# Batch normalisation of 32 x 256 x 128 x 128: two neighbouring channels per partition, 64 KB rows and a three-slot buffer

## Chip, cores, metric

One core of one Trainium2 chip. The metric is the device time of one execution in microseconds. This program runs on one core.

## The reference

```python
x: (32, 256, 128, 128) float32;  gamma, beta, running_mean, running_var: (256,)
out = gamma * (x - mean) / np.sqrt(var + 1e-5) + beta     # per channel
```

Mean and variance are inputs, so for each channel this is one multiplication and one addition. 537 MB are read and 537 MB are written.

## The kernel before

Scale and bias are worked out once per channel tile of 128 channels. The main loop then moves tiles of 128 partitions x 8192 elements (32 KB a partition, 4 MB in all) through three buffers. ScalarE does the multiplication and addition in place. SyncE issues all transfers: an issue takes it 0.34 to 0.45 us in the main loop, and the transfer is carried out later by 16 DMA engines (a load lands 22.5 us after its issue on median). The code below is cut (`...`) and its calls are drawn together on one line.

```python
x_v = x.rearrange("n (ct p) h w -> n ct p (h w)", p=P)     # channel = ct * 128 + p
...
for ct in range(c_tiles):                    # 2: eight parameter loads of 128 x 1
    nc.sync.dma_start(out=g_sb, in_=g_v[ct].unsqueeze(1))
    ...                                      # beta, mean, variance; then scale and bias
CHUNK = 8192                                 # 32 KB a partition (worked out in the kernel)
pool = ctx.enter_context(tc.tile_pool(name="sbuf", bufs=3))
for ni in range(n):
    for ct in range(c_tiles):
        for ck in range(num_chunks):         # 2
            t = pool.tile([P, CHUNK], f32, tag="t")
            nc.sync.dma_start(out=t, in_=x_v[ni, ct, :, lo:hi])                 # L88
            nc.scalar.activation(out=t, in_=t, func=Ident, bias=bias_sb, scale=scale_sb)   # L89
            nc.sync.dma_start(out=out_v[ni, ct, :, lo:hi], in_=t)               # L96
```

The scheduler of the language chooses the order in which SyncE issues these transfers. It is not the order of the loop, as the timeline below shows.

## Time and profile before

| | |
|---|---|
| time, median of 5 | 2520.67 us (2517.77 to 2531.01) |
| span of the profiled run | 2516.0 us |
| DMA queue | 99.9% of 16 engines' span, 427 GB/s |
| ScalarE | 37% busy |
| VectorE | 0% busy |

These lines are from the page of the kernel before: busy time by engine, GB/s in 40 slices of the span, the DMA queue's share, the costliest group of instructions, and the DMA issues with their size and the median time from issue to landing.

```profile
span 2516.0 us, 713 instructions
DVE 1.5 (0%) x10; ACT 924.8 (37%) x131; POOL 0.2 (0%) x4
...
GB/s 392 432 427 431 421 431 428 431 433 427 431 425 426 426 432 429 429 426 425 433 426 425 431 428 425 425 425 426 425 433 425 426 433 425 426 433 427 432 429 413
...
q1 hardware_dynamic: 38016, 1073.76, 99.9%
...
L89 ACT ACTIVATE t<-t,bias_sb,scale_sb 128x8192 f32<-128x8192 f32 x128 | 923.2, 7212 | 1573.5 <-DMA t<-in_x_dram 1573.5
...
t<-in_x_dram SPq DMA_DIRECT2D x128, 4096.0 KB, 22.5
out_dram<-t SPq DMA_DIRECT2D x128, 4096.0 KB, 12.2
```

From the first packet of x, 5.5 us into the span, the DMA engines are recorded busy practically all the time (99.9%). In the main loop ScalarE waits for loads and for nothing else (1573.5 us in 128 waits). And a store lands 12.2 us after its issue, although its own bytes take 9.7 us (8 packets of 1213 ns on each engine).

SyncE's timeline of the kernel before (start, duration, engine, line, operation, tile; SPq is SyncE; a merged line spans first to last):

```profile
3.52 0.43 SPq L53 DMA_DIRECT2D m_sb<-in_running_mean_dram  x1
4.00 0.43 SPq L54 DMA_DIRECT2D v_sb<-in_running_var_dram  x1
4.47 0.91 SPq L88 DMA_DIRECT2D t<-in_x_dram  x2
24.09 9.96 SPq L96 DMA_DIRECT2D out_dram<-t  x2
34.10 2.40 SPq L88 DMA_DIRECT2D t<-in_x_dram  x2
```

The order is two loads, two stores, two loads. The parameter loads take SyncE until 4.47 us.

Below the views lie the packet records: a packet is here one record of the DMA trace, a piece of a transfer on one engine. 94% of the 32 KB packets took 1213 ns, within 5 ns. What packets took above that is called **excess** below: summed and divided by 16 engines. In this profile it was 26.5 us.

### The profile page before, as it was taken

The page shows a single profiled execution, that of the slowest core. Times are in us where ns is not written, and L with a number is a line of the kernel's source. Part 1 is how long each engine was busy: PE and PEld are TensorE (multiplying, and loading weights), DVE is VectorE, ACT ScalarE, POOL GpSimd, SP SyncE. Part 2 cuts the span into 40 slices and gives each one's busy share as a digit, 9 for nine tenths or more (in the row PEclk, how much of TensorE's full clock was granted, in tenths as well). Part 3 has the DMA queues.
Part 4 walks back from the last instruction along what each step waited for, and adds up shares of the span by engine and source line. Part 5 has one row for each costly group of instructions (what it writes and reads, how often), then busy time and mean ns, then how long its engine had stood idle before and what let it go on. Part 6 is the DMA issues. An engine that isn't in the chain of part 4 may idle for free.

```text
span 2516.0 us, 713 instructions
## 1 busy us (share of the span) xinstructions
DVE 1.5 (0%) x10; ACT 924.8 (37%) x131; POOL 0.2 (0%) x4
## 2 busy tenths in 40 slices
DVE  0000000000000000000000000000000000000000
ACT  3342433424334243342433433334243342332433
POOL 0000000000000000000000000000000000000000
DMA  9999999999999999999999999999999999999999
GB/s 392 432 427 431 421 431 428 431 433 427 431 425 426 426 432 429 429 426 425 433 426 425 431 428 425 425 425 426 425 433 425 426 433 425 426 433 427 432 429 413
DMA packets 38021, 1073.80 MB, mean 427 GB/s; under 512 B 5248, under 2 KB 5248, under 8 KB 5248
## 3 DMA queue, kind: packets, MB, share of 16 engines
q1 hardware_dynamic: 38016, 1073.76, 99.9%
q14 instruction: 5, 0.04, 0.0%
HBM read 536.88 MB, written 536.87 MB: 427 GB/s over the span
## 4 chain that ended last, share of the span: by engine, by line
DMA 80%; ACT 18%; SPq 1%; issue 0%; ACTq 0%
DMA t<-in_x_dram 65%; ACT t L89 18%; DMA out_dram<-t 15%; SPq L96 0%; ACTq L89 0%; SPq L54 0%; SPq L53 0%; SPq L52 0%; SPq L51 0%; SPq L88 0%
## 5 line engine op out<-in xcount | busy, mean ns | idle before, releaser
L89 ACT ACTIVATE t<-t,bias_sb,scale_sb 128x8192 f32<-128x8192 f32 x128 | 923.2, 7212 | 1573.5 <-DMA t<-in_x_dram 1573.5
L60 ACT ACTIVATE v_sb<-v_sb 128x1 f32<-128x1 f32 x2 | 0.4, 202 | 4.0 <-DVE v_sb L59 4.0
L60 ACT ACT_TABLE_LOAD x1 | 1.3, 1283 | 0.7 <-PEq L111 0.7
L61 DVE RECIPROCAL v_sb<-v_sb 128x1 f32<-128x1 f32 x2 | 0.3, 164 | 0.3 <-ACT v_sb L60 0.3
L64 DVE TENSOR_TENSOR bias_sb<-b_sb,m_sb 128x1 f32<-128x1 f32 x2 | 0.3, 159 | 0.1
L63 DVE TENSOR_TENSOR m_sb<-m_sb,scale_sb 128x1 f32<-128x1 f32 x2 | 0.3, 159 | 0.0
L62 DVE TENSOR_TENSOR scale_sb<-g_sb,v_sb 128x1 f32<-128x1 f32 x2 | 0.3, 158 | 0.1
L59 DVE TENSOR_SCALAR v_sb<-v_sb 128x1 f32<-128x1 f32 x2 | 0.3, 154 | 5.3 <-DMA v_sb<-in_running_var_dram 5.3
L111 POOL MEMSET const-bfloat16-1.0<- 128x1 bf16 x1 | 0.1, 101 | 0.0
L111 POOL MEMSET const-uint8-127<- 128x1 uint8 x1 | 0.1, 101 | 0.0
L111 POOL MEMSET const-float32-0.0<- 128x1 f32 x1 | 0.1, 98 | 0.2 <-issue 0.2
L111 POOL MEMSET const-float32-1.0<- 128x1 f32 x1 | 0.1, 98 | 0.0
## 6 DMA issues: line engine op xcount, KB each, us to landing
t<-in_x_dram SPq DMA_DIRECT2D x128, 4096.0 KB, 22.5
out_dram<-t SPq DMA_DIRECT2D x128, 4096.0 KB, 12.2
g_sb<-in_gamma_dram SPq DMA_DIRECT2D x2, 0.5 KB, 2.0
b_sb<-in_beta_dram SPq DMA_DIRECT2D x2, 0.5 KB, 2.1
m_sb<-in_running_mean_dram SPq DMA_DIRECT2D x2, 0.5 KB, 2.0
v_sb<-in_running_var_dram SPq DMA_DIRECT2D x2, 0.5 KB, 2.0
```

What stands on the lines that cost most here:

```text
L59: nc.vector.tensor_scalar_add(out=v_sb, in0=v_sb, scalar1=float(eps))
L60: nc.scalar.sqrt(out=v_sb, in_=v_sb)
L61: nc.vector.reciprocal(out=v_sb, in_=v_sb)
L62: nc.vector.tensor_mul(out=scale_sb, in0=g_sb, in1=v_sb)
L63: nc.vector.tensor_mul(out=m_sb, in0=m_sb, in1=scale_sb)
L64: nc.vector.tensor_sub(out=bias_sb, in0=b_sb, in1=m_sb)
L89: nc.scalar.activation(out=t, in_=t, func=Ident, bias=bias_sb, scale=scale_sb,)
L111: nc = _bacc.Bacc("TRN2", target_bir_lowering=False, num_devices=1)
```

## The change

The intent is longer contiguous rows, fewer and larger transfers, and fewer parameter loads. Channels 2p and 2p+1 go to partition p, so one partition's two channels are 128 KB in a row in memory. Three slots of 64 KB a partition replace three buffers of 32 KB. Where two adjacent slots are next, a whole image (16 MB) loads in one transfer. Otherwise its two channel tiles load one by one.

```diff
-    g_v = gamma.rearrange("(ct p) -> ct p", p=P)
+    g_v = gamma.rearrange("(p ct) -> p ct", p=P)
     ... (beta, mean, variance likewise)
+    x_v = x.rearrange("n (p ct) h w -> n ct p (h w)", p=P)
+    out_v = out.rearrange("n (p ct) h w -> n ct p (h w)", p=P)
-    for ct in range(c_tiles):
-        g_sb = scratch.tile([P, 1], f32, tag=f"g{ct}")
-        nc.sync.dma_start(out=g_sb, in_=g_v[ct].unsqueeze(1))
+    g_sb = scratch.tile([P, c_tiles], f32, tag="g")
+    nc.sync.dma_start(out=g_sb, in_=g_v)
     ... (four parameter loads in place of eight; same arithmetic on 128 x 2)
-    pool = ctx.enter_context(tc.tile_pool(name="sbuf", bufs=3))
+    NSLOTS = 3
+    pool = ctx.enter_context(tc.tile_pool(name="sbuf", bufs=1))
+    big = pool.tile([P, NSLOTS, hw], f32)
+    x_p = x.rearrange("n (p two) h w -> n p (two h w)", two=2)
+    slot = 0
     for ni in range(n):
+        if slot + 2 <= NSLOTS:
+            t = big[:, slot:slot + 2, :]
+            nc.sync.dma_start(out=t, in_=x_p[ni].rearrange("p (two m) -> p two m", two=2))
+            for ct in range(2):
+                nc.scalar.activation(out=big[:, slot + ct, :], ...)      # 128 x 16384
+                nc.sync.dma_start(out=out_v[ni, ct], in_=big[:, slot + ct, :])
+            slot = (slot + 2) % NSLOTS
+        else:
+            for ct in range(2):
+                ...    # load, activation, store of one slot (the very last one in two halves)
+                slot = (slot + 1) % NSLOTS
```

More of the change, by code (lines that the diff above doesn't have):

```diff
@@ L31 @@
     out_v = out.rearrange("n (ct p) h w -> n ct p (h w)", p=P)
-    g_v = gamma.rearrange("(ct p) -> ct p", p=P)
-    b_v = beta.rearrange("(ct p) -> ct p", p=P)
-    rm_v = running_mean.rearrange("(ct p) -> ct p", p=P)
-    rv_v = running_var.rearrange("(ct p) -> ct p", p=P)
+    g_v = gamma.rearrange("(p ct) -> p ct", p=P)
+    b_v = beta.rearrange("(p ct) -> p ct", p=P)
+    rm_v = running_mean.rearrange("(p ct) -> p ct", p=P)
+    rv_v = running_var.rearrange("(p ct) -> p ct", p=P)
+    x_v = x.rearrange("n (p ct) h w -> n ct p (h w)", p=P)
+    out_v = out.rearrange("n (p ct) h w -> n ct p (h w)", p=P)
     f32 = mybir.dt.float32
@@ L41 @@
     scratch = ctx.enter_context(tc.tile_pool(name="scratch", bufs=1))
-    scale_aps = []
-    bias_aps = []
-    for ct in range(c_tiles):
-        g_sb = scratch.tile([P, 1], f32, tag=f"g{ct}")
-        b_sb = scratch.tile([P, 1], f32, tag=f"b{ct}")
-        m_sb = scratch.tile([P, 1], f32, tag=f"m{ct}")
-        v_sb = scratch.tile([P, 1], f32, tag=f"v{ct}")
-        nc.sync.dma_start(out=g_sb, in_=g_v[ct].unsqueeze(1))
-        nc.sync.dma_start(out=b_sb, in_=b_v[ct].unsqueeze(1))
-        nc.sync.dma_start(out=m_sb, in_=rm_v[ct].unsqueeze(1))
-        nc.sync.dma_start(out=v_sb, in_=rv_v[ct].unsqueeze(1))
-        scale_sb = params.tile([P, 1], f32, tag=f"scale{ct}")
-        bias_sb = params.tile([P, 1], f32, tag=f"bias{ct}")
-        nc.vector.tensor_scalar_add(out=v_sb, in0=v_sb, scalar1=float(eps))
-        nc.scalar.sqrt(out=v_sb, in_=v_sb)
-        nc.vector.reciprocal(out=v_sb, in_=v_sb)
-        nc.vector.tensor_mul(out=scale_sb, in0=g_sb, in1=v_sb)
-        nc.vector.tensor_mul(out=m_sb, in0=m_sb, in1=scale_sb)
-        nc.vector.tensor_sub(out=bias_sb, in0=b_sb, in1=m_sb)
-        scale_aps.append(scale_sb)
-        bias_aps.append(bias_sb)
@@ L69 @@
-    CHUNK = hw
-    MAX_BYTES_PER_PART = 32 * 1024
-    while CHUNK * 4 > MAX_BYTES_PER_PART:
-        CHUNK //= 2
-    assert hw % CHUNK == 0
-    num_chunks = hw // CHUNK
-    pool = ctx.enter_context(tc.tile_pool(name="sbuf", bufs=3))
+    g_sb = scratch.tile([P, c_tiles], f32, tag="g")
+    b_sb = scratch.tile([P, c_tiles], f32, tag="b")
+    m_sb = scratch.tile([P, c_tiles], f32, tag="m")
+    v_sb = scratch.tile([P, c_tiles], f32, tag="v")
+    nc.sync.dma_start(out=g_sb, in_=g_v)
+    nc.sync.dma_start(out=b_sb, in_=b_v)
@@ new lines @@
+    nc.sync.dma_start(out=m_sb, in_=rm_v)
+    nc.sync.dma_start(out=v_sb, in_=rv_v)
+    scale_full = params.tile([P, c_tiles], f32, tag="scale")
+    bias_full = params.tile([P, c_tiles], f32, tag="bias")
+    nc.vector.tensor_scalar_add(out=v_sb, in0=v_sb, scalar1=float(eps))
+    nc.scalar.sqrt(out=v_sb, in_=v_sb)
+    nc.vector.reciprocal(out=v_sb, in_=v_sb)
+    nc.vector.tensor_mul(out=scale_full, in0=g_sb, in1=v_sb)
+    nc.vector.tensor_mul(out=m_sb, in0=m_sb, in1=scale_full)
+    nc.vector.tensor_sub(out=bias_full, in0=b_sb, in1=m_sb)
@@ L78 @@
+    scale_aps = [scale_full[:, ct:ct + 1] for ct in range(c_tiles)]
+    bias_aps = [bias_full[:, ct:ct + 1] for ct in range(c_tiles)]
+    assert c_tiles == 2, "optimized for 256 channels"
+    NSLOTS = 3
+    pool = ctx.enter_context(tc.tile_pool(name="sbuf", bufs=1))
+    big = pool.tile([P, NSLOTS, hw], f32)
     Ident = mybir.ActivationFunctionType.Identity
+    x_p = x.rearrange("n (p two) h w -> n p (two h w)", two=2)
+    out_p = out.rearrange("n (p two) h w -> n p (two h w)", two=2)
+    slot = 0
@@ L80 @@
     for ni in range(n):
-        for ct in range(c_tiles):
-            scale_sb = scale_aps[ct]
-            bias_sb = bias_aps[ct]
-            for ck in range(num_chunks):
-                lo = ck * CHUNK
-                hi = lo + CHUNK
-                t = pool.tile([P, CHUNK], f32, tag="t")
-                nc.sync.dma_start(out=t, in_=x_v[ni, ct, :, lo:hi])
+        if slot + 2 <= NSLOTS:
+            t = big[:, slot:slot + 2, :]
+            nc.sync.dma_start(out=t, in_=x_p[ni].rearrange("p (two m) -> p two m", two=2))
+            for ct in range(2):
@@ L89 @@
                 nc.scalar.activation(
-                    out=t,
-                    in_=t,
+                    out=big[:, slot + ct, :],
+                    in_=big[:, slot + ct, :],
                     func=Ident,
-                    bias=bias_sb,
-                    scale=scale_sb,
-                )
-                nc.sync.dma_start(out=out_v[ni, ct, :, lo:hi], in_=t)
+                    bias=bias_aps[ct],
+                    scale=scale_aps[ct],
+                )
+                nc.sync.dma_start(out=out_v[ni, ct], in_=big[:, slot + ct, :])
@@ new lines @@
+            slot = (slot + 2) % NSLOTS
+        else:
+            for ct in range(2):
+                s = slot
+                pieces = 2 if ni == n - 1 and ct == 1 else 1
+                step = hw // pieces
+                for lo in range(0, hw, step):
+                    part = big[:, s, lo:lo + step]
+                    nc.sync.dma_start(out=part, in_=x_v[ni, ct, :, lo:lo + step])
+                    nc.scalar.activation(
+                        out=part,
+                        in_=part,
+                        func=Ident,
+                        bias=bias_aps[ct],
+                        scale=scale_aps[ct],
+                    )
+                    nc.sync.dma_start(out=out_v[ni, ct, :, lo:lo + step], in_=part)
+                slot = (slot + 1) % NSLOTS
```

## The prediction

The sum of 23 us still counts the step that is cut, 8 us for longer packets, beside 13 us for the turns and 1.9 us for the parameter loads; the terms left come to about 15 us. The "no 8 us" and the 2418 ns further down come from the cut step too; 2418 ns is also what the trace then showed.

> **What bounds the kernel now.** Moving bytes. The page's queue part: packets of the hardware DMA queue fill 99.9% of 16 engines' span; the slices show 427 GB/s on average (1073.7 MB in 2516 us). ScalarE is busy 923 us (37%), and the waits put all its idle time (1573.5 us) down to loads. That costs nothing while the DMA queue has work. SyncE's timeline: two loads, two stores, two loads; each store goes out just before the queue would run dry.
>
> The packet records show what is left to gain. 32,768 packets carry 32 KB each; nearly all take 1213 ns, so 16 engines move 432 GB/s when nothing disturbs them. [...] The mean packet takes 1226 ns: the excess sits in the last packets of a store that a load follows (1573 ns, +0.36 us; 64 such places, about 20 us). Before the first load, SyncE spends 4.5 us, most of it on eight parameter loads, 0.47 us each.
>
> **What the change does.**
> - Same bytes. Channels 2p and 2p+1 sit on partition p, so a whole image loads as one 16 MB transfer, rows of 128 KB; 64 activations of 16384 elements, about 14.2 us each (estimate from 7.21 us for 8192 and 0.20 us for one). ScalarE stays near 915 us, hidden.
> - [...]
> - Turns from store to load: with three 8 MB slots I expect a period of three images: pair load, single load, three stores, single load, pair load, three stores. That is 2 turns per three images, about 21 against 64: -13 us (estimate).
> - Four parameter loads fewer before the first load of x: -1.9 us.
> - The first activation waits 39 us, but the next load fills the queue meanwhile: 0.
>
> **Does the pipeline hold?** A pair lands, ScalarE needs 14.2 us plus about 2 us of landing and issue before the store goes out; behind the pair another 8 MB transfer (19.4 us) must be queued. In the order above it is: margin about 3 us. The last channel tile is cut in two 4 MB pieces so that its activation (7.2 us) hides as before.
>
> **Sum.** 23 us off the span, all on the critical path, since the queue is the path. Time 2498 us (-0.9%), range 2484 to 2520. Chances: faster by over 2% 0.05, within 2% 0.86, slower by over 2% 0.09.
>
> **What would show it.** Right: DMA share 99% or more, mean near 431 GB/s, about 16,384 packets of 64 KB at about 2418 ns, slow packets only at some 21 turns, first x load issued near 2.6 us, about 43 loads and 65 stores. Wrong step: 32 KB packets (no 8 us); slow packets that grow with size, or elsewhere (no 13 us); slices with DMA share under 9 (pipeline broken).
>
> **What would make it wrong.** A store that waits for an activation issued before a ready load: a gap of some 16 us each, ten to thirty times (2650 us and up). A dependency tracked over the whole three-slot tile: far slower. Rows 128 KB apart in HBM being slower than 64 KB apart.

## More of the kernel before

What SyncE waits for in the kernel before (waiter, awaited, total us, times, longest):

```profile
SPq L96 <- ACT t L89: 2300.5, 128, 27.5
SPq L88 <- DMA out_dram<-t: 92.9, 63, 1.5
```

Every store waits for its activation, and 63 loads wait a little (1.5 us at most) for a finished store that frees their buffer.

## The result, and the profile after

The median was 2492.99 us (2491.08 to 2495.61, 9 runs) against 2520.45 us (16 runs of the kernel before). The ratio is 0.9892, 95% interval 0.9875 to 0.9908. A ratio is the mean time of one kernel's fast runs over that of the other's of the same rounds, so it is not quite the ratio of the medians quoted.

The same lines of the page of the changed kernel:

```profile
span 2491.8 us, 340 instructions
DVE 0.8 (0%) x5; ACT 896.9 (36%) x67; POOL 0.2 (0%) x4
...
GB/s 404 438 436 424 437 438 432 430 433 437 436 436 427 433 437 434 425 437 437 422 438 436 423 438 436 423 438 434 424 437 432 427 438 433 425 438 431 427 434 395
...
q1 hardware_dynamic: 18960, 1073.75, 99.9%
...
L83 ACT ACTIVATE big<-big,bias_full,scale_full 128x16384 f32<-128x16384 f32 x42 | 587.4, 14032 | 979.0 <-DMA big<-in_x_dram 979.0
...
out_dram<-big SPq DMA_DIRECT2D x63, 29.9
big<-in_x_dram SPq DMA_DIRECT2D x42, 58.0
```

The share of the DMA queue is 99.9% as before, so that number cannot tell where 24 us went. Half as many packets moved the same bytes. An 8 MB store now lands 29.9 us after its issue, and its own bytes take 19.3 us (8 packets of 2418 ns on each engine). On median 10.6 us are left for other work ahead of it (and for landing), where the kernel before had 2.5.

SyncE's timeline of the changed kernel:

```profile
2.10 0.43 SPq L52 DMA_DIRECT2D v_sb<-in_running_var_dram  x1
2.58 0.43 SPq L81 DMA_DIRECT2D big<-in_x_dram  x1
3.05 0.47 SPq L99 DMA_DIRECT2D big<-in_x_dram  x1
58.03 14.27 SPq L90 DMA_DIRECT2D out_dram<-big  x2
85.89 0.33 SPq L107 DMA_DIRECT2D out_dram<-big  x1
86.33 0.73 SPq L99 DMA_DIRECT2D big<-in_x_dram  x1
```

The order is two loads (a pair and a single one), three stores, two loads: 21 turns from store to load in the whole run, against 63 before.

The difference of the two profiled spans, worked out from the packet records:

| | before | after | difference |
|---|---|---|---|
| span start to first packet of x | 5.5 us | 3.7 us | -1.9 |
| all packets at their usual length (1213 ns for 32 KB; 2418 ns for 64 KB), per engine | 2484.2 | 2476.2 | -8.1 |
| excess | 26.5 | 11.2 | -15.3 |
| rest (overlapping records, last landing) | -0.2 | 0.8 | +1.0 |
| span | 2516.0 | 2491.8 | -24.2 |

The three terms of the prediction's sum (1.9 us, 13 us and the 8 us) seem to be found, one by one. The experiments show that the largest of them has another cause than the one predicted.

### The profile page after: what moved, and what is told of

Same layout as the page of the kernel before. It is cut to its first block, busy times and chain, and to the rows that moved or that the text cites. A ratio compares the mean times of both kernels' runs of the same rounds, so it can differ in the third digit from the quotient of the medians.

```text
span 2491.8 us, 340 instructions
## 1 busy us (share of the span) xinstructions
DVE 0.8 (0%) x5; ACT 896.9 (36%) x67; POOL 0.2 (0%) x4
## 3 DMA queue, kind: packets, MB, share of 16 engines
q1 hardware_dynamic: 18960, 1073.75, 99.9%
## 4 chain that ended last, share of the span: by engine, by line
another core or an unknown queue 60%; ACT 25%; issue 11%; DMA 3%; SPq 0%; ACTq 0%
ACT big L83 12%; ACT big L100 12%; DMA big<-in_x_dram 3%; ACTq L83 0%; SPq L52 0%; SPq L51 0%; SPq L50 0%; SPq L49 0%; SPq L107 0%; ACTq L100 0%
## 5 line engine op out<-in xcount | busy, mean ns | idle before, releaser
L83 ACT ACTIVATE big<-big,bias_full,scale_full 128x16384 f32<-128x16384 f32 x42 | 587.4, 14032 | 979.0 <-DMA big<-in_x_dram 979.0
L100 ACT ACTIVATE big<-big,bias_full,scale_full 128x16384 f32<-128x16384 f32 (+1 forms) x23 | 309.1, 13438 | 600.1 <-DMA big<-in_x_dram 600.1
## 6 DMA issues: line engine op xcount, KB each, us to landing
out_dram<-big SPq DMA_DIRECT2D x63, 29.9
```

The costliest lines, as they stand in the source:

```text
L83: nc.scalar.activation(out=big[:, slot + ct, :], in_=big[:, slot + ct, :], func=Ident, bias=bias_aps[ct], scale=scale_aps[ct],)
L100: nc.scalar.activation(out=part, in_=part, func=Ident, bias=bias_aps[ct], scale=scale_aps[ct],)
```

## The experiments

My first theory was that packets have a fixed part (64 KB in one packet took 8 ns less than in two: 2418 against 2 x 1213 ns), and, as in the prediction, that each *turn* of the queue from store to load costs some 0.39 us (24.4 us of excess around 63 turns before). The rivals were that the layout or the size of the transfers is what counts. Each kernel was timed in five rounds beside the kernel before. Three chips were used, one for e1 to e4, one for e5 to e8 and one for e9 to e12; each ratio is to the kernel before in the same rounds on the same chip. Span, excess and turns are those of one profiled execution, which in e2, e4, e7 and e9 was the slowest of those timed.

| run | ratio to before (95%) | median us | profiled span us | excess us | turns store to load |
|---|---|---|---|---|---|
| before, first profile | 1 | 2520.67 | 2516.0 | 26.5 | 63 |
| e1 changed kernel again | 0.9912 (0.9898, 0.9926) | 2494.67 | 2491.9 | 11.4 | 21 |
| e2 32 KB packets | 0.9933 (0.9921, 0.9945) | 2498.94 | 2499.7 | 13.0 | 21 |
| e3 layout only | 0.9976 (0.9963, 0.9989) | 2510.78 | 2508.7 | 20.7 | 63 |
| e4 8 MB tiles | 0.9949 (0.9933, 0.9964) | 2502.18 | 2507.7 | 22.8 | 31 |
| e5 before again | 0.9995 (0.9977, 1.0014) | 2515.72 | 2515.6 | 25.3 | 63 |
| e6 one in turn, 3 ahead | 0.9898 (0.9881, 0.9915) | 2492.22 | 2490.5 | 3.1 | 125 |
| e7 two in turn, 3 ahead | 0.9901 (0.9883, 0.9919) | 2492.16 | 2494.0 | 2.8 | 63 |
| e8 four in turn | 0.9895 (0.9875, 0.9915) | 2491.53 | 2489.8 | 2.4 | 31 |
| e9 two in turn, 2 ahead | 1.0015 (0.9999, 1.0032) | 2523.15 | 2524.6 | 29.1 | 63 |
| e10 before, work split | 0.9963 (0.9945, 0.9980) | 2509.83 | 2508.1 | 18.8 | 63 |
| e11 changed, work split | 0.9887 (0.9871, 0.9903) | 2490.52 | 2488.5 | 4.9 | 21 |
| e12 three in turn | 0.9944 (0.9931, 0.9958) | 2505.23 | 2503.4 | 6.0 | 21 |

### e1: the changed kernel again

No edit; it stands on the chip beside e2 to e4.

> The changed kernel, unaltered, so that the runs beside it have it on the same chip. Every theory: about 2493 us, ratio to before about 0.989, span about 2492 us, 21 turns from store to load, 11 us of packet excess.

Measured: as expected, 21 turns and 11.4 us of excess.

### e2: the changed kernel with packets of 32 KB

```diff
-    big = pool.tile([P, NSLOTS, hw], f32)
+    big = pool.tile([P, NSLOTS, 2, HALF + PAD], f32)     # HALF = 8192, PAD = 16 elements
     ... (all views end in [..., :HALF]; same transfers in the same order)
```

> The changed kernel with 64 bytes of padding after every 32 KB of a row in SBUF, so that no packet can be longer than 32 KB; same transfers, same order, same turns. My theory (a fixed part of 8 ns in every packet): 32,768 packets of 1213 ns, 8 us slower than the changed kernel on the same chip, about 2501 us; the excess at turns unchanged near 10 us. Rival (the gain comes with the large transfers or the layout, and the packet's size matters nothing): same as the changed kernel, 2493 us. Rival (packets carry most of the gain): 2512 us or more.

Measured: 32,768 packets of 1213 ns. The profiled span is 7.8 us longer than e1's, and the median 4.3 us longer. All six executions of e2 (2498.38 us and up) were slower than all five of e1 (up to 2495.15). Two packets of 32 KB take 2 x 1213 - 2418 = 8 ns more than one of 64 KB, and 1024 such pairs on each engine make 8 us. So this term of the prediction's sum is real, at 4 to 8 us. Why the longer packet takes less the trace doesn't show.

### e3: the layout alone

```diff
-    x_v = x.rearrange("n (ct p) h w -> n ct p (h w)", p=P)
+    x_v = x.rearrange("n (p ct) h w -> n ct p (h w)", p=P)
     ... (out and the four parameters likewise)
```

> The kernel before with channels 2p and 2p+1 on partition p (so rows of one transfer start 128 KB apart), nothing else: 4 MB transfers, 32 KB packets, two loads and two stores in turn, eight parameter loads of 4-byte elements 8 bytes apart. My theory: no part of the gain, 2520 us as before (ratio 1.000, within 0.3%), 63 turns of 0.39 us. Rival (the rows' place in HBM makes the transfers faster): up to the whole gain, ratio near 0.99.

Measured: 0.24% faster, and the interval excludes 1. This lies within the 0.3% that I had allowed around 1.000, but it is some 5 us where I had expected no part of the gain. The order, the packets and the 63 turns are those of before; only the excess is smaller. The control e5, on another chip, shows the usual excess (25.3 us), so the kernel's own spread is an unlikely reason. The trace fits what is called lead below: only 5 of e3's 63 turns came after a second store with less than 1.2 us of lead, against 15 in the kernel before and 14 in e5, and at equal lead a turn loses about the same. Why the layout makes late stores rarer stays open.

### e4: tiles of 8 MB in the kernel before

```diff
-    MAX_BYTES_PER_PART = 32 * 1024
+    MAX_BYTES_PER_PART = 64 * 1024
```

> The kernel before with one size changed: tiles of 64 KB a partition in place of 32 KB, so 64 loads and 64 stores of 8 MB, order two loads, two stores, 31 turns from store to load, 64 KB packets; layout and eight parameter loads as before. My theory: -8 us from the packets and about -12 us from half of the turns, so 2500 us, ratio about 0.992, if every store is issued before the queue is dry (the activation of 14 us must fit under the load behind it, 19 us: it does). Rival (layout or the 16 MB pair load is needed): 2510 us or more.

Measured: the time fits (2502.18 us), but the reason doesn't. With half the turns the excess was 22.8 us and not 12. This is of the slowest of six executions (2509.46 us), and some 13 us of it lie around the 31 turns from store to load, as the theory had it; another 7 us lie around the turns from load to store. (The 0.7 us a turn that e8's expectation takes from here counts all of the excess.) But by quarters of the run the excess was 3.1, 6.3, 6.7 and 6.7 us, and a turn from store to load cost nothing in the first cycles and some 0.6 us later. A cost per turn would be the same in each quarter. This was the first sign against the turn theory.

### e5: the kernel before again

No edit; a control.

> The kernel before, unaltered, as a control: how far two copies of it differ in paired rounds, and how its packet excess varies from profile to profile. Every theory: ratio 1.000 within 0.3%, 63 turns with 20 to 25 us of excess. If the excess is as low as the 20.7 us that the run with the layout alone showed, then that run's gain of 0.24% was the kernel's own spread and not the layout.

Measured: ratio 0.9995, excess 25.3 us.

### e6, e7, e8: the number of turns by itself

Six slots of 32 KB a partition in place of three, and the order of issue on SyncE written out. Layout, 4 MB transfers, 32 KB packets and parameter loads stay those of before.

```diff
+    SLOTS = 6; RUN = 1        # e6; 2 in e7, 4 in e8
+    for _ in range(AHEAD):    # loads issued before the first store: 3 (4 in e8)
+        load(loads.pop(0))
+    while stores:
+        for _ in range(min(RUN, len(stores))):
+            store(stores.pop(0))
+        for _ in range(min(RUN, len(loads))):
+            load(loads.pop(0))
```

> The kernel before with six 32 KB slots and the order of issue on SyncE written out: three loads ahead, then one store, one load, one store: about 125 turns from store to load in place of 63; layout, 4 MB transfers, 32 KB packets and parameter loads as before. My theory (each turn costs some 0.39 us): excess near 50 us, time about 25 us above the kernel before, ratio 1.010. Rival (the excess belongs to the bytes, or to something that happens now and then, not to the turns): excess 20 to 26 us, ratio 1.000.

> The same six slots and written order with two stores and two loads in turn: 62 or 63 turns. Both theories: as the kernel before, ratio 1.000 (a control for the six slots and for loads that are queued earlier). If it is faster than before, then the depth of the queue matters, not the turns.

> The same with four stores and four loads in turn: 31 turns. My theory: excess near 12 us, 12 us below the run with two in turn, ratio about 0.995. Rival (excess not tied to turns): ratio 1.000. Third possibility, suggested by the run with 8 MB tiles, whose 31 turns cost 0.7 us each: the cost of a turn grows with the bytes written before it; then the excess stays near 20 us.

Measured: all three gain 1%, with 125, 63 or 31 turns alike. In e6 the packets around all 125 turns from store to load together have 0.1 us of excess, where the kernel before had 24.4 us at its 63. **The turn theory falls.** A turn by itself is free here. The sentence put down for e7, that a gain there would mean that the depth of the queue matters, applies.

The page of e6 (span, GB/s by slice, time from issue to landing):

```profile
span 2490.5 us, 587 instructions
...
GB/s 385 431 433 430 434 433 432 435 433 434 432 435 432 435 432 432 435 432 434 433 434 432 435 432 433 434 432 435 432 435 432 435 432 434 433 430 435 432 435 406
...
out_dram<-big SPq DMA_DIRECT2D x128, 4096.0 KB, 41.2
```

A store now lands 41.2 us after its issue, for 9.7 us of bytes. It stands long in the queue, and this is good: between the first slice and the last the rate stays at 430 to 435 GB/s, and the excess is 3.1 us.

**The new theory: lead.** Call *lead* the time from a transfer's issue on SyncE to the start of its first packets (taken from the trace, mean over 16 engines). Each transfer leaves 16 completions in the trace (4224 for 264 transfers in the kernel before). In the kernel before, an activation started 0.07 us (median) after the last of the 16 completions of its load, and its store was issued 0.03 us after the activation's end. Only the rest of the next load (9.7 us) is in the queue meanwhile, and landing plus 7.2 us of activation use up nearly all of it. In this kernel's profile, set the lead of the second store of each pair against the excess at the turn that follows:

| lead of the second store | cycles | mean lead us | mean excess at the next turn us |
|---|---|---|---|
| under 1.2 us | 15 | 1.03 | 0.74 |
| 1.2 to 1.5 | 8 | 1.35 | 0.49 |
| 1.5 to 1.7 | 24 | 1.61 | 0.29 |
| over 1.7 | 16 | 1.79 | 0.15 |

The correlation is -0.99 (e5 and e9 also -0.99). The line reaches zero at a lead of about 2 us. So the loss is recorded at the turn, which is why I took the turn for its cause, but its size goes with how late the store before was issued. That it follows from it is for e9 and e10 to show.

### e9: the lead alone

```diff
-    AHEAD = 3
+    AHEAD = 2          # in e7's kernel; nothing else
```

> The six-slot kernel with two stores and two loads in turn, but two loads ahead of the stores in place of three: the order is then the kernel before's (two loads, two stores), still six slots and no wait of SyncE for a finished store. New theory (what costs is the lead: how long before the queue runs dry a store is issued; the second store needs about 2 us, and the kernel before gives it 1.0 to 1.8 us): leads of 1 to 2 us again, excess back near 25 us, ratio to before 1.000. Rival (six slots in place of three, or SyncE's waits for finished stores, made the difference): excess 3 us, ratio 0.990.

Measured: one load fewer ahead, and the whole percent is gone: ratio 1.0015, median lead of the stores 1.6 us. The two kernels' pages, e7 first, then e9:

```profile
span 2494.0 us, 587 instructions
...
out_dram<-big SPq DMA_DIRECT2D x128, 4096.0 KB, 23.4
```

```profile
span 2524.6 us, 587 instructions
...
out_dram<-big SPq DMA_DIRECT2D x128, 4096.0 KB, 12.3
```

What SyncE waits for in e9:

```profile
SPq L100 <- ACT big L96: 2358.5, 128, 28.4
SPq L137 <- DMA out_dram<-big: 11.5, 2, 9.6
```

No load waits for a finished store here (the two waits of L137 are at the program's end), and there are six slots. So neither the slots nor those waits were the cause in the kernel before. What e9 takes away is one load queued ahead, and with it the lead; e10 changes the lead and leaves the loads ahead as they were.

### e10: the kernel before, with the activation split between two engines

```diff
-                nc.scalar.activation(out=t, in_=t, func=Ident, bias=bias_sb, scale=scale_sb)
+                nc.scalar.activation(out=t[:, :half], in_=t[:, :half], ...)
+                nc.vector.tensor_scalar(out=t[:, half:], in0=t[:, half:], scalar1=scale_sb,
+                                        scalar2=bias_sb, op0=mult, op1=add)
```

> The kernel before with half of each tile's columns done by VectorE (multiply and add) in place of ScalarE: the store can go out some 3.5 us earlier, so its lead is about 5 us in place of 1.0 to 1.8; three slots, order, turns, packets and waits for finished stores stay. Lead theory: excess falls from 25 us to about 3 us, 63 turns notwithstanding; ratio about 0.991, 2494 us. Rivals (turns; number of slots; SyncE's waits for finished stores; ScalarE is hidden and cannot matter): ratio 1.000.

Measured: ScalarE takes 3.80 us for its half of a tile and VectorE 2.41 us, in place of 7.21 us for the whole. The direction is right, since ScalarE, 37% busy and "hidden", did cost time. But less than half of the expected gain came (0.4%). Its GB/s by slice, from the page:

```profile
GB/s 385 433 431 432 434 434 432 432 432 434 433 434 432 432 433 429 430 430 427 427 431 430 427 427 427 433 427 429 431 427 427 429 432 427 427 432 428 426 427 397
```

After the first slice it runs at 431 to 434 for a third of the run, and then falls to between 426 and 433 until the last slice. Meanwhile the 16 DMA engines drift apart. To see it, take the time from the first to the last of the 16 completions of one transfer. Mean by sixths of the run, for loads:

| | 1st | 2nd | 3rd | 4th | 5th | 6th | leads of stores |
|---|---|---|---|---|---|---|---|
| before | 0.8 us | 0.8 | 0.9 | 0.9 | 0.9 | 0.8 | 1.0 to 1.8 us |
| e10 | 0.8 | 2.4 | 3.9 | 4.0 | 4.0 | 4.0 | 5.1 us at first, median 2.3 |
| changed kernel | 0.9 | 2.1 | 3.1 | 3.4 | 3.3 | 3.6 | first store of a pair: 5.5 us at first, 1.9 to 2.8 in the second half |
| e8 | 1.0 | 2.3 | 3.0 | 3.0 | 3.0 | 3.0 | 19 us |
| e11 | 0.7 | 2.2 | 3.4 | 4.0 | 5.2 | 6.7 | first store of a pair: 8 to 9 us in mid-run |

(In e7 it was 6.9 us in the last sixth.) While e10's lead was 4 to 5 us, its turns from store to load had no excess at all. The activations start on the last of a load's 16 completions, so I take the drift to come off the lead: as e10's spread grew from 0.8 to 4.0 us, its lead fell from 5.1 us to a median of 2.3. When the lead was down to about 2 us, the losses of the kernel before came back (excess by quarter: 2.5, 3.9, 6.4, 6.0 us). I had expected that 5 us of lead would last; more than half of it was gone. The lead below which losses begin isn't one number, either: e10's turns lost 0.4 us at a mean lead of 2.0 us, 0.3 us at 2.2 and nothing above 2.6, where the kernel before lost only 0.15 us at 1.8. A mean over 16 engines that are 4 us apart may hide those that run dry first; this was not tested.

### e11: the changed kernel, with the activation split

```diff
+    def affine(t, ct):        # half of the columns on ScalarE, half on VectorE, as in e10
-                nc.scalar.activation(out=big[:, slot + ct, :], ...)
+                affine(big[:, slot + ct, :], ct)
```

> The changed kernel with the same split between ScalarE and VectorE: leads of its stores grow from 2 to 5 us by some 7 us. Lead theory: its excess of 11 us falls to about 3 us, so 2485 us, ratio about 0.987 to before. Rival (the rest of its excess belongs to its 21 turns or to its large transfers): unchanged 2493 us.

Measured: excess 4.9 us in place of 11.2, span 3.3 us shorter, with the same 21 turns and the same transfers. The lead theory's direction holds: most of the rest of the changed kernel's excess goes when stores are issued earlier. Not all of it lies beside a late store, though: about 4.5 us of the changed kernel's 11.2 lie in the 16 MB loads that are queued behind a single load, and the store after them has some 22 us of lead. In e11 they hold 0.8 us. Why the loss lies there is open. The time, 2490.52 us, is 5 us short of the hoped 2485. The engines drift to 6.7 us here; whether that is what is missing was not shown. In the same rounds as the kernel before it is at 0.9887; the changed kernel has 0.9892 and 0.9912 in others. So a gain over the changed kernel is small, if any, and was not measured side by side.

### e12: three loads and three stores in turn, parameters on another queue

```diff
-    nc.sync.dma_start(out=g_sb, in_=g_v)
+    nc.scalar.dma_start(out=g_sb, in_=g_v)           # all four parameters
     ...
+    # single 8 MB loads; order on SyncE written out: L L L S S S
```

> A version meant to beat both: the changed kernel's three slots, layout and 64 KB packets, but single 8 MB loads in place of pairs, three loads and three stores in turn (order written out), and the parameter loads on ScalarE's queue. Every store and load then has some 20 us or more of lead without help from VectorE, and the first load of x is issued near 0.7 us in place of 2.6. Lead theory: excess about 3 us, about 2 us less before the first load: 2483 us, ratio about 0.986. Rival (the pair load is what helps): 2495 us or more.

Measured: 2505.23 us, 22 us more than I expected, and by its number on the side of the rival. The order did what it should (stores have some 21 us of lead, excess 6.0 us). My other edit spoiled the start. Timeline of e12 (ACTq is ScalarE as issuer of transfers):

```profile
0.73 1.32 SPq L100 DMA_DIRECT2D big<-in_x_dram  x3
...
2.13 0.86 ACTq L52 DMA_DIRECT2D v_sb<-in_running_var_dram  x1
...
62.07 0.17 DVE L57 TENSOR_SCALAR v_sb<-v_sb 128x2 f32<-128x2 f32 x1 [62.07 <-DMA v_sb<-in_running_var_dram]
...
63.30 41.90 ACT L101 ACTIVATE big<-big,bias_full,scale_full 128x16384 f32<-128x16384 f32 x3 [0.82 <-DVE bias_full L62]
```

Windows of e12 (stretch, us, busy time of VectorE, ScalarE, GpSimd, clock, DMA share, GB/s):

```profile
61.00:79.00 18.00, 0.82 (x5) 15.91 (x3) 0.00 (x0) 1.00 0.14 58
```

The parameter loads of 1 KB, issued at 0.7 to 2.1 us on the second queue, landed 22, 41, 60 and 60 us later: the first three each behind about one more 8 MB load (19.3 us), the fourth with the third. In the changed kernel the same four loads, issued by SyncE ahead of the loads of x, landed 1.7 to 1.8 us after issue. So small loads on a second queue can wait out whole transfers of the first; how the engines take turns between the two queues the trace doesn't show. The first activation started at 63.3 us, and the DMA queue stood nearly empty from 61 to 79 us (DMA share 0.14). The step between the starts of neighbouring packets there is 17.1 us too long. With that taken off the span, e12 would be near 2486 us; this is an estimate, and that version was not run, so the rival is not refuted by a run.

## Why the prediction was right, and where it was not

- **Bound by moving bytes, gain under 2%: right.** The queue is at 99.9% in both, and the changed kernel moves 431 GB/s over its span. What the traces show: with all packets at their usual length the bytes take 2484.2 us in 32 KB packets and 2476.2 us in the changed kernel's, 1.3% and 1.6% less than the span before (2516.0 us), and no run came under 2488 us of span.
- **Packets, -8 us: right in size.** There are 16,128 packets of 64 KB at 2418 ns, as forecast to the nanosecond, and 512 of 32 KB. The packet records give -8.1 us. Taking the long packets away (e2) costs 4.3 us by the medians and 7.8 us by the profiled spans.
- **Fewer parameter loads, -1.9 us: right.** The first load of x is issued at 2.58 us in place of 4.47.
- **Order and number of transfers: right.** Two loads and three stores in turn, 44 loads (43 forecast), 65 stores, 21 turns, and no large gap.
- **Turns from store to load, 0.39 us each, -13 us: wrong as a cause, near in size by luck.** The excess fell by 15.3 us, but not because turns became fewer: 125 turns cost nothing in e6 (0.1 us), and 63 cost next to nothing in e7 (2.8 us of excess in all). Around the turns from store to load it fell by 21 us (24.4 to 3.2), more than 42 turns at 0.39 us explain, and 7.1 us came up around the turns from load to store, which held 0.5 us before; the two together happen to be near 13. In place of this step stands lead. The changed kernel doubles both the activation and the transfer that hides it, and so what remains between them. After the first load lands, 19.3 us of the next are in the queue against 14 us of activation, where it was 9.7 against 7.2. The first store of a pair had 5.5 us of lead at first and 1.9 to 2.8 in the second half, in place of 1.0 to 1.8; the prediction's margin of about 3 us was near that. e9 against e7 shows the cause by itself: the same number of turns, slots and packets, one load less ahead, 31 us more (ratios 1.0015 and 0.9901 to the kernel before, each on its own chip). In e10 the loads ahead stay as they were, and the turns lose nothing while the lead is long.
- **"That costs nothing while the DMA queue has work": wrong.** The prediction even read that each store goes out just before the queue would run dry, and did not ask how long before is long enough. e10 shows that a faster activation on an engine that is 37% busy gains 0.4%.
- **"Slow packets only at some 21 turns": only partly right.** In the changed kernel the turns from store to load hold 3.2 us of the excess, and those from load to store 7.1 us.
- **The layout, counted as 0: too low by itself.** e3 gained 0.24% from it. How much of that is in the changed kernel's 15 us can't be told from these runs, since its leads are longer anyway.

What stays open: why about 2 us of lead are needed, and more in e10. A first load needs 1.1 us from the start of its issue to its first packets (4.47 to 5.5 us). It is also open why the lost time is recorded in the last packets before the turn rather than where the late store begins, why the engines drift, and why they stop at 3.0 us in e8 but reach 6.7 us in e11.

## What to carry to other kernels

A DMA queue that shows 99.9% busy can still lose a percent (here 26.5 us of excess in 2516): compare the median time from issue to landing with the time that the bytes alone take. If the difference is only 2 or 3 us, as here (12.2 against 9.7 us; 41.2 against 9.7 us in e6), transfers may be issued too late. Then try one more load ahead of the stores (31 us here, e7 against e9), or a quicker step between load and store (0.4% in e10), before larger transfers (here 32 KB packets with three loads ahead did as well as 64 KB packets with a pair load: ratios 0.9901 and 0.9892). A cost that always sits at one place in the trace is not yet caused by what happens at that place: vary the number of those places before you build on it.
